# A batched matrix product in groups of four: neighbours, or one matrix from each quarter of the batch

## Chip, core and metric

The kernel runs on one core of a Trainium2 chip. The core has compute engines that run side by side: PE (matrix products and transposes), DVE (vector copies and casts), ACT (copies and casts as well), and POOL, which here only builds an identity matrix. SP does no arithmetic; it issues the transfers between the device's memory and the core's own memory, SBUF. Sixteen DMA engines carry the transfers out. SBUF has 128 partitions, and a tile is 128 rows, one in each partition. The metric is the device time in microseconds; less is better.

## The reference

128 independent products (8 x 16 matrices), each of a 256 x 512 matrix x with a 512 x 384 matrix of weights, all float32:

```python
b1, b2, m, k, n = 8, 16, 256, 512, 384
x:      (b1, b2, m, k)
weight: (b1, b2, k, n)

def reference(x, weight):
    return np.matmul(x, weight).astype(np.float32)
```

The kernel reads 67.1 MB of x and 100.7 MB of weights and writes 50.3 MB of output.

## The kernel before

The 128 matrices are taken in NG = 32 groups of G = 4. A group of before is four neighbours in memory. Three kinds of transfer serve one group:

- two weight loads, for two matrices each: 1,024 rows of weights stand one behind the other in memory and are cut into 128 runs of 8 rows (8 x 384 x 4 = 12,288 bytes), one run to a partition of `w_sb` (lines 103 to 108);
- one load of x: 1,024 rows, cut into 128 runs of 8 rows (8 x 512 x 4 = 16,384 bytes), into `x_sb` (lines 111 to 114);
- one store of the output, of 128 runs of 8 rows (8 x 384 x 4 = 12,288 bytes), from `out_sb` (line 122). The last group's store is cut in four pieces.

Thus partition p of `x_sb` has rows of matrix p // 32 of the group, and partition p of a weight slot has rows of matrix p // 64 of its pair.

The order is written out by hand. Each engine has its own program, and semaphores tie them together. SP (`on_sync`) issues the loads of the first four groups, then in turn the loads of group n + 4 and the store of group n. Before each it waits until the buffer is free: a weight slot when DVE has cast it (`w_cast`, line 102), an x slot when ACT has cast it (`x_cast`, line 110), and before a store until ACT has written the output tile (`o_copied`, line 121). There are 4 weight slots (two groups), 2 slots of x and 4 of output. A load into one of them can be issued as soon as the group two earlier has been cast.

ACT casts x to bfloat16 (`cast_x`, line 132), PE transposes it (line 166), DVE casts the weights (line 147) and copies the transposes out of PE's accumulation memory (line 153), PE multiplies (line 180) and ACT copies the product to `out_sb` (line 194). ACT's first copy of a group waits until the store of four groups earlier has read that output tile (`o_out`, line 192).

The lines that the change touches make the patterns of the transfers. The left one is in SBUF, the right one in memory:

```python
x_rows = x.rearrange("b1 b2 m k -> (b1 b2 m) k")
x_sb[s % XS][:]
x_rows[bass.ds(n * (G * M), G * M)].rearrange("(p r) k -> p r k", r=R)
```

A partition's rows follow each other on both sides, so the program has [128 runs, 4096 numbers] on each side of the load of x, and [128, 3072] on each side of the loads of weights and of the whole stores.

Of the kernel before, what the change touches and what calls it, by code (L numbers as in the profile page):

```python
# [12 lines left out]
def kernel(  # L13
# [9 lines left out]
    b1, b2, M, K = x.shape  # L23
    _, _, _, N = weight.shape
    B = b1 * b2
    KO = K // P

    x_rows = x.rearrange("b1 b2 m k -> (b1 b2 m) k")
    w_rows = weight.rearrange("b1 b2 k n -> (b1 b2 k) n")
    o_rows = out.rearrange("b1 b2 m n -> (b1 b2 m) n")  # L30

    fp32 = mybir.dt.float32
    bf16 = mybir.dt.bfloat16

# [5 lines left out]
    G = 4  # L40
    C = P // G
    R = G * M // P
    T = R // 2
    D = 2
    S = 2
    HP = P // D
    NG = B // G

    XS, WS, OS = 2, 2 * G // D, 4
    BS, TS, WBS = 1, 2, 2 * G  # L50
# [6 lines left out]
    def sbuf(name, shape, dtype, n):  # L57
        return [
            ctx.enter_context(nc.sbuf_tensor(f"{name}{s}", shape, dtype)) for s in range(n)
        ]  # L60
# [6 lines left out]
    def sems(name, n):  # L67
        return [tc.alloc_semaphore(f"{name}{s}") for s in range(n)]
# [3 lines left out]
    x_sb = sbuf("x_sb", [P, R, K], fp32, XS)  # L72
# [3 lines left out]
    w_sb = sbuf("w_sb", [P, S * KO, N], fp32, WS)  # L76
    w_bf = sbuf("w_bf", [P, KO, N], bf16, WBS)
    out_sb = sbuf("out_sb", [P, R, N], fp32, OS)
# [12 lines left out]
    x_in, w_in, o_out = sems("x_in", XS), sems("w_in", WS), sems("o_out", OS)  # L91
# [5 lines left out]
    def load(e, t, U, s):  # L97
        n = t * U + s
        for d in range(G // D):
            slot = (s * (G // D) + d) % WS  # L100
            if not isinstance(n, int) or n >= 2:
                e.wait_ge(w_cast, n * (G * S) + ((d + 1) * D * S - 2 * G * S))
            e.dma_start(  # L103
                w_sb[slot][:],
                w_rows[bass.ds(n * (G * K) + d * (D * K), D * K)].rearrange(
                    "(p k) n -> p k n", k=S * KO
                ),
            ).then_inc(w_in[slot], 16)
        if not isinstance(n, int) or n >= XS:
            e.wait_ge(x_cast, n * T + (1 - XS) * T)  # L110
        e.dma_start(  # L111
            x_sb[s % XS][:],
            x_rows[bass.ds(n * (G * M), G * M)].rearrange("(p r) k -> p r k", r=R),
        ).then_inc(x_in[s % XS], 16)

    def store(e, t, U, s, pieces=1):
        n = t * U + s
        dram = o_rows[bass.ds(n * (G * M), G * M)].rearrange("(p r) n -> p r n", r=R)
        for q in range(pieces):
            rows = slice(q * R // pieces, (q + 1) * R // pieces)  # L120
            e.wait_ge(o_copied, n * T + ((q + 1) * T // pieces + BIAS))
            e.dma_start(out=dram[:, rows], in_=out_sb[s % OS][:, rows]).then_inc(
                o_out[s % OS], 16
            )

    def cast_x(e, t, U, s, q):
        n = t * U + s
# [77 lines left out]
    def on_sync(e):  # L205
        U = OS
        for n in range(LAG):
            load(e, 0, NG, n)
        rounds = (NG - LAG) // U
        with e.Fori(0, rounds) as t:  # L210
            for s in range(U):
                load(e, t, U, LAG + s)
                store(e, t, U, s)
        for n in range(rounds * U, NG):
            if n + LAG < NG:
                load(e, 0, NG, n + LAG)
            store(e, 0, NG, n, T if n == NG - 1 else 1)
        for s in range(OS):
            e.wait_ge(o_out[s], 16 + 16 * (NG // OS + (T - 1 if s == (NG - 1) % OS else 0)))
# [67 lines left out]
```

## Time and profile before

| | |
|---|---|
| median of 3 runs | 518.51 us (518.35 to 518.73) |
| the profiled execution, whole | 518.98 us |
| its span, from the first to the last instruction | 517.2 us |
| moved | 218.18 MB, 422 GB/s over the span |
| PE busy | 306.6 us (59%) |
| DVE busy | 332.8 us (64%) |
| ACT busy | 236.7 us (46%) |

Times of the profile are those of one execution. A percentage is a share of the span. In the view of slices, the span is cut into 40 equal parts, and a digit is the busy share of a part in tenths, 9 for 90% or more; the row "DMA" is the mean over the sixteen DMA engines. A packet is what a DMA engine moves in one piece. In rows of waits, the engine and line that wait stand on the left, what ended the wait on the right, and then the time in total, the number of times and the longest. In rows of issues, the last number is the median time from the issue of a transfer to its landing. L103 is line 103 of the kernel before.

### The profile page before, as it was taken

How to read it: one execution, taken by the hardware profiler on the slowest of the kernel's cores; microseconds unless marked ns; L12 is line 12 of the kernel's file. 1: busy time of each engine (PE TensorE's matmuls, PEld its weight loads, DVE VectorE, ACT ScalarE, POOL GpSimd, SP SyncE). 2: the span in 40 equal slices, each digit the busy share in tenths (PEclk: the TensorE clock that was granted, in tenths of full speed). 3: DMA queues.
4: the chain of work that ended last, by engine and by line, in shares of the span. 5: the costliest groups of instructions: out<-in, count | busy, mean ns of one | idle time of the engine just before them, and what ended most of it. 6: DMA issues, size and time to landing. Idle time of an engine off the chain costs nothing.

```text
span 517.2 us, 11523 instructions
## 1 busy us (share of the span) xinstructions
PE 306.6 (59%) x4608; PEld 200.6 (39%) x4608; DVE 332.8 (64%) x384; ACT 236.7 (46%) x264; POOL 0.7 (0%) x6
## 2 busy tenths in 40 slices
PE   0478776556665457645577554776446765467752
PEld 0345444334443334433344332444324443244431
DVE  3698875667556676556675566855658656676550
ACT  0465564443644436435355354454444544544441
POOL 0000000000000000000000000000000000000000
PEclk9998877878777887878777778877788877778777
DMA  8999999999999999999999999999999999999996
GB/s 340 430 423 424 424 432 426 429 428 430 432 427 427 427 428 432 429 427 430 426 431 431 426 429 430 427 432 427 427 429 429 427 433 425 430 428 430 429 428 251
DMA packets 18869, 218.18 MB, mean 422 GB/s; under 512 B 2096, under 2 KB 2096, under 8 KB 2608
## 3 DMA queue, kind: packets, MB, share of 16 engines
q1 hardware_dynamic: 18864, 218.11, 99.3%
q8 instruction: 3, 0.05, 0.0%
q14 instruction: 2, 0.02, 0.0%
HBM read 167.77 MB, written 50.33 MB: 422 GB/s over the span
## 4 chain that ended last, share of the span: by engine, by line
DMA 81%; ACT 10%; PE 4%; issue 3%; ACTq 0%; SPq 0%
DMA x_sb<-in_x_dram 81%; ACT x_bf L132 9%; PE po L180 2%; PE pt L166 1%; ACTq L130 0%; ACT out_sb L194 0%; SPq L111 0%; SPq L103 0%; ACT L132 0%; ACTq L193 0%; SPq L282 0%; SPq L55 0%
## 5 line engine op out<-in xcount | busy, mean ns | idle before, releaser
L147 DVE CAST w_bf<-w_sb 64x1536 bf16<-64x1536 f32 x256 | 244.4, 955 | 47.2 <-DMA w_sb<-in_weight_dram 38.5
L166 PE MATMUL pt<-identity,x_bf 128*128 128x128 f32 x512 | 123.7, 425 | 199.3 <-ACT x_bf L132 199.1
L180 PE MATMUL po<-w_bf,x_t 128*32 128x384 bf16 x4096 | 185.1, 342 | 1.0 <-issue 1.0
L166 PEld LDWEIGHTS pt<-identity,x_bf 128*128 128x128 f32 x512 | 91.8, 216 | 232.1 <-issue 218.3
L194 ACT COPY out_sb<-po 128x768 f32<-128x768 f32 x128 | 102.2, 798 | 147.2 <-PE po L180 147.2
L153 DVE COPY x_t<-pt 128x1024 bf16<-128x1024 bf16 x128 | 88.4, 691 | 122.3 <-PE pt L166 121.8
L132 ACT CAST x_bf<-x_sb 128x1024 bf16<-128x1024 f32 x128 | 124.4, 1042 | 80.9 <-DMA x_sb<-in_x_dram 80.8
L180 PEld LDWEIGHTS po<-w_bf,x_t 128*32 128x32 bf16 x4096 | 108.8, 101 | 73.8 <-issue 14.2
L132 ACT ACT_TABLE_LOAD x8 | 10.3, 1283 | 42.9 <-DMA x_sb<-in_x_dram 42.9
masks.py:199 POOL TENSOR_SCALAR_AFFINE_SELECT identity<-identity 128x128 f32<-128x128 f32 x1 | 0.3, 292 | 0.2 <-POOL identity L200 0.2
L200 POOL MEMSET identity<- 128x128 f32 x1 | 0.2, 204 | 0.5 <-SPq L55 0.5
L271 POOL MEMSET const-bfloat16-1.0<- 128x1 bf16 x1 | 0.1, 101 | 0.0
L271 POOL MEMSET const-uint8-127<- 128x1 uint8 x1 | 0.1, 101 | 0.0
L271 POOL MEMSET const-float32-0.0<- 128x1 f32 x1 | 0.1, 98 | 0.2 <-issue 0.2
L271 POOL MEMSET const-float32-1.0<- 128x1 f32 x1 | 0.1, 98 | 0.0
## 6 DMA issues: line engine op xcount, KB each, us to landing
w_sb<-in_weight_dram SPq DMA_DIRECT2D x64, 1536.0 KB, 27.5
x_sb<-in_x_dram SPq DMA_DIRECT2D x32, 2048.0 KB, 27.5
out_dram<-out_sb SPq DMA_DIRECT2D x31, 1536.0 KB, 30.7
out_dram<-out_sb SPq DMA_DIRECT2D x4, 384.0 KB, 5.9
```

Source lines behind the costliest of these rows:

```text
L132: e.copy(out=x_bf[s % BS][:, rows], in_=x_sb[s % XS][:, rows].rearrange("p r (q s c) -> p r s q c", s=S, c=KO),).then_inc(x_cast, 1)
L147: e.tensor_copy(out=w_bf[(s * G + d * D + a) % WBS][h * HP : (h + 1) * HP], in_=w_sb[slot][a * HP : (a + 1) * HP, h * KO : (h + 1) * KO, : ...
L153: e.tensor_copy(out=x_t[s % TS][:, 2 * q : 2 * q + 2], in_=pt[(s * T + q) % PT][:].bitcast(bf16),).then_inc(t_copied, 1)
L166: ins = e.transpose(pt[(s * T + q) % PT][:, rr, h, :], words[:, 2 * q + rr, h :: KO // 2], identity[:],)
L180: ins = e.matmul(po[(s * T + q) % PO][mine, rr, :N], x_t[s % TS][:, 2 * q + rr, ko // 2, mine, ko % 2], w_bf[(s * G + i) % WBS][:, ko, :], ...
L194: e.copy(out=out_sb[s % OS][:, 2 * q : 2 * q + 2, :], in_=po[(s * T + q) % PO][:, :, :N],).then_inc(o_copied, 1)
L200: e.memset(identity[:], 0.0).then_inc(id_done, 1)
L271: nc = _bacc.Bacc("TRN2", target_bir_lowering=False, num_devices=1)
```

## The change

A group is now made of matrices n, n + 32, n + 64 and n + 96, one from each quarter of the batch. The memory of x, weights and output is named in four dimensions (quarter i, group n, run within the matrix, bytes of the run), and a transfer takes all quarters (for weights: two of four) at one n. The runs of a matrix keep their length and partition; only which matrices stand in a group is new, and where the transfers go in memory. The quarters begin 16.8 MB apart in x, 25.2 MB in the weights and 12.6 MB in the output. The product, the casts, the waits and the order of issues are as they were; the lines after the new ones move down by up to seven.

```diff
-    x_rows = x.rearrange("b1 b2 m k -> (b1 b2 m) k")
-    w_rows = weight.rearrange("b1 b2 k n -> (b1 b2 k) n")
-    o_rows = out.rearrange("b1 b2 m n -> (b1 b2 m) n")
...
+    x_runs = x.rearrange("b1 b2 m k -> (b1 b2 m) k").rearrange(
+        "(i n c r) k -> i n c (r k)", i=G, n=NG, r=R
+    )
+    w_runs = weight.rearrange("b1 b2 k n -> (b1 b2 k) n").rearrange(
+        "(i n p k) f -> i n p (k f)", i=G, n=NG, k=S * KO
+    )
+    o_runs = out.rearrange("b1 b2 m n -> (b1 b2 m) n").rearrange(
+        "(i n c r) f -> i n c (r f)", i=G, n=NG, r=R
+    )
...
             e.dma_start(
-                w_sb[slot][:],
-                w_rows[bass.ds(n * (G * K) + d * (D * K), D * K)].rearrange(
-                    "(p k) n -> p k n", k=S * KO
+                w_sb[slot][:].rearrange("p k n -> p (k n)"),
+                w_runs[d * D : (d + 1) * D, bass.ds(n, 1)].rearrange(
+                    "i n p f -> i (n p) f"
                 ),
             ).then_inc(w_in[slot], 16)
...
         e.dma_start(
-            x_sb[s % XS][:],
-            x_rows[bass.ds(n * (G * M), G * M)].rearrange("(p r) k -> p r k", r=R),
+            x_sb[s % XS][:].rearrange("p r k -> p (r k)"),
+            x_runs[:, bass.ds(n, 1)].rearrange("i n c f -> i (n c) f"),
         ).then_inc(x_in[s % XS], 16)
...
-        dram = o_rows[bass.ds(n * (G * M), G * M)].rearrange("(p r) n -> p r n", r=R)
+        dram = o_runs[:, bass.ds(n, 1)].rearrange("i n c f -> i (n c) f")
         for q in range(pieces):
-            rows = slice(q * R // pieces, (q + 1) * R // pieces)
+            run = slice(q * R * N // pieces, (q + 1) * R * N // pieces)
             e.wait_ge(o_copied, n * T + ((q + 1) * T // pieces + BIAS))
-            e.dma_start(out=dram[:, rows], in_=out_sb[s % OS][:, rows]).then_inc(
-                o_out[s % OS], 16
-            )
+            e.dma_start(
+                out=dram[:, :, run],
+                in_=out_sb[s % OS][:].rearrange("p r n -> p (r n)")[:, run],
+            ).then_inc(o_out[s % OS], 16)
```

## The prediction

> **What bounds the kernel now.** I read the slices of the page first, then the DMA queues, one stretch of the middle, the waits of the queue that issues the transfers (SP), and the issues. The slices, with the queue under them:
>
> ```profile
> DMA  8999999999999999999999999999999999999996
> GB/s 340 430 423 424 424 432 426 429 428 430 432 427 427 427 428 432 429 427 430 426 431 431 426 429 430 427 432 427 427 429 429 427 433 425 430 428 430 429 428 251
> DMA packets 18869, 218.18 MB, mean 422 GB/s; under 512 B 2096, under 2 KB 2096, under 8 KB 2608
> ## 3 DMA queue, kind: packets, MB, share of 16 engines
> q1 hardware_dynamic: 18864, 218.11, 99.3%
> ```
>
> The sixteen DMA engines are full from the first slice to the last but one, so the time is bytes over engines. I take one price from these lines: 99.3% of 16 engines over 517.2 us is 8217 engine-us for 218.11 MB, or 37.67 engine-us per MB (26.5 GB/s for one engine). A row of 12,288 B then holds its engine for 0.463 us, one of 16,384 B for 0.617 us. The work of one engine of the sixteen is 8217/16 = 513.6 us; the span has 3.6 us besides, for start and end. One stretch of the middle, two groups long (columns: busy us of PE, PE loads, DVE, ACT and POOL with counts, clock, DMA share, GB/s), says the same without the ends:
>
> ```profile
> 200.00:264.00 64.00, 39.01 (x582) 25.39 (x584) 41.76 (x50) 29.60 (x33) 0.00 (x0) 0.79 1.01 429
> ```
>
> 429 GB/s over 16 is 26.8 GB/s an engine, and DVE, the busiest of the compute engines, works 41.8 of 64 us. The packet count shows how a transfer is cut: 64 weight loads, 32 x loads and 35 stores are 131 transfers; at 128 rows each that is 16,768 packets, and the 2096 under 512 B are 131 x 16, one completion from each of sixteen engines. 16,768 + 2096 = 18,864, the queue's count. So a packet is one row of one partition, and every transfer is shared by all sixteen engines, 8 rows each.
>
> ```profile
> SPq L103 <- DVE w_bf L147: 269.5, 60, 8.6
> SPq L111 <- ACT x_bf L132: 122.5, 30, 5.6
> SPq L122 <- ACT out_sb L194: 35.5, 6, 16.2
> ```
>
> (waits of SP's queue: us in total, times, longest) and, from the issues (KB each, median us from issue to landing):
>
> ```profile
> w_sb<-in_weight_dram SPq DMA_DIRECT2D x64, 1536.0 KB, 27.5
> x_sb<-in_x_dram SPq DMA_DIRECT2D x32, 2048.0 KB, 27.5
> out_dram<-out_sb SPq DMA_DIRECT2D x31, 1536.0 KB, 30.7
> ```
>
> SP waits for buffers to be emptied by the casts, and still a transfer takes 27.5 us from issue to landing although its own 8 rows need 3.7 us: it stands behind some two groups of other transfers. That backlog is why SP's waits cost nothing.
>
> [...] a transfer issued from SP runs on k engines, [...] The trace before agrees for 128 against 128: k = 16, by the 2096 completions. No trace before shows a smaller k. [...]
>
> **The change part by part.** Instruction order and counts of PE, DVE, ACT and SP stay as they are; the built program differs in the shapes of the transfers alone. Bytes and row sizes stay too: 12,288 B rows of weight and output, 16,384 B rows of x. Costs nothing: which four matrices make a group, since no instruction of the casts, transposes or products sees it.
>
> What changes is the pattern on the DRAM side. Four matrices of four quarters don't follow each other in memory, so the rows no longer make one dimension of 128. The weight load is [2, 64, 3072] against [128, 1, 3072] in SBUF, the x load [4, 32, 4096] against [128, 1, 4096], the store [4, 32, 3072] against [128, 3072]. [...] k is 2 for the weight loads, 4 for x loads and stores. Engines 0 and 1 then carry half of every weight load and a quarter of everything else; 2 and 3 a quarter of x and output; twelve carry nothing. For engine 0:
>
> - weights: 64 loads x 64 rows = 4096 rows, 50.33 MB x 37.67 = 1896 us
> - x: 32 loads x 32 rows = 1024 rows, 16.78 MB x 37.67 = 632 us
> - output: a quarter of 50.33 MB, 12.58 MB x 37.67 = 474 us
> - sum 79.69 MB, 3002 us, against 513.6 now.
>
> Does engine 0 stay full? A group is 59.3 + 19.8 + 14.8 = 93.8 us of it. From the rows of the page, DVE needs 8 x 0.955 + 4 x 0.691 = 10.4 us a group, ACT 4 x (1.042 + 0.798) = 7.4, PE 306.6/32 = 9.6. A weight slot is cast within 4 x 0.955 us and its next load issued while the other slots' loads, worth more than 60 us, wait behind the engine. So compute hides under the transfers, and SP's waits still cost nothing, longer as they get. Twelve idle engines hide nothing, since no row may move to them. At the end, the last x share is followed on engine 0 by four stores of 14.8 us; the last group's compute takes 11 us (first cast at 496.66, last copy out at 507.72), and its first copy out waits for the first of those stores (four output buffers); so the last pieces join before the engine runs dry. Start and end stay 3.6 us: span 3006.
>
> An unknown: [...] Bounds: from below nothing, if an engine's own pace is the limit or they don't meet. From above, engines 0 and 1 in step through all x and output rows, each at half pace: 632 + 474 = 1106 us more. I take one meeting a group, costing engine 1 once [...] 4 x 0.463 = 1.85 us, 32 times, 59 us. [...] Another unknown is the pace of an engine alone: the best slice, 433 GB/s or 27.1 an engine, makes 2945 of the 3002[...].
>
> Sum: 3006 + 59 = 3065 for the span. The profiled execution took 518.98 for a span of 517.2, 1.8 around it; its 518.98 stands 0.5 above the median of 518.51, which at this size is nothing. Forecast 3067 us.
>
> **The rivals.**
> - *All sixteen engines stay* (not slower). Place: the cut of a transfer into shares. If the 128 partitions on the SBUF side alone decide it, or the two DRAM dimensions are walked as one before sharing, each engine keeps 8 rows and 513.6 us; price nothing, time 518.5. For it: packets follow partitions today, and the rows keep their size. [...] It decides if the x loads show 16 completions. 4 in 100.
> - *Sixteen engines, but far regions collide in HBM* [...] The quarters lie 16.8 MB apart in x, 25.2 in weights, 12.6 in output. At half rate: 2 x 513.6 + 5.4, about 1033 us. Against: inside a quarter 32 or 64 rows follow each other[...]. 3 in 100.
> - *In step [...]*: above 3350, up to 3006 + 1106 + 2 = 4114 us. For it: engines 0 and 1 get the same list at the same time. Against: nothing holds them in step. 8 in 100.
> - *Shares handed out one engine after the other*: [...] nearly all 218.11 MB go in series, up to 8217 us. The trace shows only shares of 8 rows, so it can't exclude this. 2 in 100.
> - *A lone engine is faster than 26.8 GB/s*, if today's pace is a share of a common limit: at twice the pace, 1500 us. Against: the slices hold 423 to 433 whatever mix of loads and stores they have. 2 in 100.
>
> **How the numbers follow.** The forecast's own case [...] has 81 in 100: from 2950 (best slice's pace, no meeting) to 3350 (a quarter of the in-step cost, 277, over the 59). The rest lies outside, 8 above [...], 2 far above, 9 below; so the range is 2950 to 3350. A measurement here tells 0.2% from no change. Slower: 81 + 8 + 3 + 2 + 2 = 96. Of the rival with sixteen engines 3 are within 0.2%, and 1 is faster, by some packets that wait less.
>
> **What would show it.** In the changed profile: DMA share near 3002 x 2 + (632 + 474) x 2 over 16 x 3065, some 17% (tenths of 1 or 2); about 71 GB/s; completions of 64 x 2 + 67 x 4 = 396 in place of 2096, so about 17,170 packets in all; weight loads landing 100 us or more after issue; DVE busy the same 333 us but 11% of the span. Wrong would be 2096 completions (then a sixteen-engine rival), a DMA share well under 17% (shares in series, or an engine that runs dry), or a queue time per MB far from 37.67 ([...] a faster lone engine).

## The result, and the profile after

The changed kernel took 3352.85 us (3335.56 to 3375.89, six runs) where the kernel before took 518.29 in the runs beside it: 6.4686 times as long, 95% interval 6.4408 to 6.4965. The forecast was 3067, its range 2950 to 3350. The direction and the main cause were right; a term beside the main sum was too small by a factor of six to seven, and the time lies just past the end of the range.

From the page of the changed kernel, the slices and the queue under them:

```profile
DMA  1111111211111111221112111111111121111121
GB/s 61 61 65 51 60 65 68 66 54 63 66 69 72 55 63 63 70 70 55 66 65 70 70 57 67 65 69 73 60 66 64 68 70 65 68 60 65 68 70 78
DMA packets 17169, 218.17 MB, mean 65 GB/s; under 512 B 396, under 2 KB 396, under 8 KB 908
## 3 DMA queue, kind: packets, MB, share of 16 engines
q1 hardware_dynamic: 17164, 218.11, 18.0%
```

The bytes are the same, but the sixteen engines are busy for 18.0% where it was 99.3%, and 422 GB/s have become 65. The packets under 512 B, the completions, went from 2096 to 396. That is exactly 64 x 2 + 67 x 4: a weight load runs on two engines, a load of x and a store on four. The page gives no time to landing for these transfers, and its chain puts 88% down to an unknown queue. As I read it, both say that the transfers' ends weren't matched; the packets are the place to look.

DVE waits for weights 2325.8 of the 3355 us, and SP no longer shows many waits (the first line is DVE's, the second SP's):

```profile
DVE w_bf L154 <- DMA w_sb<-in_weight_dram: 2325.8, 64, 44.2
```

```profile
SPq L109 <- DVE w_bf L154: 96.9, 4, 38.2
```

Before, SP waited 269.5 us at that place. It isn't free now: it is held inside the issue itself. One load of x, by its tile, before and after (min/median/max in ns):

```profile
L111 SPq DMA_DIRECT2D x_sb<-in_x_dram x32: 328/333/483, 1.9 to 468.9; - x32
```

```profile
L117 SPq DMA_DIRECT2D x_sb<-in_x_dram x32: 7337/28462/29877, 2.3 to 3188.6; - x32
```

An issue of 0.33 us has become one of 28 us. Why it takes so long the trace doesn't show; when it ends, engine 1 (as named below) has 70 to 74 rows left before its own x in twelve of the first thirteen groups. The end of the issue goes with the start on engines 2 and 3: in the first seven groups their first row of x starts 0.8 to 0.9 us after it.

What the sum of 3006 left out shows in single rows, a row being the packet of one partition. The packet records of the trace have no engine number, but each row starts where the last one on its engine ended, so they can be put into four chains. Two of them have weights and are engines 0 and 1, two have none and are engines 2 and 3. Which is which of a pair the records don't say, nor to which partitions a row goes: the numbers are names, and I call engine 1 the one whose weights are slowed. From the first twelve to thirteen groups of the changed kernel, mean ns of a row:

```
                     weights (12,288 B)   x (16,384 B)   output (12,288 B)
engine 0                  473                 614               494
engine 1                  559                 644               460
engine 2                   -                 1054               463
engine 3                   -                 1085               466
two_halves, median        460                 611               460
```

The last line is from the run on two engines below (two_halves); it stands for a row alone. Engine 1's weight rows take 99 ns longer than that; over its 4096 such rows it would be 0.41 ms. Engines 2 and 3 take 1.7 to 1.8 times as long for a row of x. Engine 0, which reads from the same far regions, loses 13 ns a weight row. It is engine 1 that sets the time: up to 1400 us its chain has gaps of 0.3 us in all, while engine 0 stands idle for 121 us. Many of the slow rows take near two or three times the time alone, others fall between. Here is the second group's second weight load on engine 1, four rows to a line (start in us, ns of each), with the x of engine 2 (or 3) beside it:

```
engine 1, second weight load                  engine 2 (or 3), x
120.60   621 1245  460  460                   117.04   869 1302  781 1199
123.37   632 1349 1367 1289                   121.18  1347 1227 1749 1828
128.00   800 1351 1349 1382                   127.32  1149 1675 1834 1552
132.87   789  945 1369 1349                   133.51  1180 1802 1628  725
137.30   954  804 1213 1349                   138.84  1079 1792 1274  611
141.61  1081  812 1053 1359                   143.58  1061 1801 1255  611
145.90  1066  468  838 1053                   148.29  1066 1628 1199  855
149.31  1066  468  460  460                   153.03   655 1211 1219  724
151.75   460  466  460  460
```

The first 32 rows took 31.2 us, where 32 x 0.457 would be 14.6 (0.457 us is the step from one start to the next). The view of the queue in that stretch, 90 to 210 us in slices of 3 us, shows it as bytes:

```profile
DMA  1111111112222221222222111111111122222222
GB/s 56 53 53 53 53 53 57 53 59 91 67 63 64 59 64 53 68 72 61 67 74 83 57 57 49 57 52 56 52 56 56 51 75 86 86 91 81 86 96 78
```

From the start two engines are busy and move 53 GB/s, 26.7 each. From the tenth slice on (117 us) it is up to four, and from 120 to 156 us they move 53 to 83, not 107. By the chains engine 0 keeps its 26.7 from 120.6 to 151.8 us, while engines 1, 2 and 3 move 12.6, 12.6 and 12.1: the three together 1.4 times what one moves alone. The next x of engines 2 and 3 begins at 188 us; there the loss is smaller (75 to 96).

The start at 117 us follows from SP. Its timeline (start and duration in us) has the issue of this load of x end at 116.2 us, and engine 2's first row of it starts at 117.0:

```profile
86.90 29.27 SPq L117 DMA_DIRECT2D x_sb<-in_x_dram  x1
```

### The profile page after: what moved, and what is told of

It is laid out like the page before. It is cut to its first block, busy times and chain, and to the rows that moved or that the text cites. A ratio compares the mean times of both kernels' runs of the same rounds, so it can differ in the third digit from the quotient of the medians.

```text
span 3355.0 us, 11523 instructions
## 1 busy us (share of the span) xinstructions
PE 365.7 (11%) x4608; PEld 224.4 (7%) x4608; DVE 332.8 (10%) x384; ACT 234.1 (7%) x264; POOL 0.7 (0%) x6
## 2 busy tenths in 40 slices
DMA packets 17169, 218.17 MB, mean 65 GB/s; under 512 B 396, under 2 KB 396, under 8 KB 908
## 4 chain that ended last, share of the span: by engine, by line
another core or an unknown queue 88%; PE 5%; ACT 4%; issue 1%; ACTq 0%; SPq 0%
PE po L187 5%; ACT x_bf L139 3%; ACT out_sb L201 1%; PE pt L173 0%; ACTq L137 0%; ACTq L200 0%; ACTq L252 0%; ACT L139 0%; ACTq L250 0%; ACTq L289 0%; SPq L61 0%; ACTq L248 0%
## 5 line engine op out<-in xcount | busy, mean ns | idle before, releaser
L154 DVE CAST w_bf<-w_sb 64x1536 bf16<-64x1536 f32 x256 | 244.4, 955 | 2331.8 <-DMA w_sb<-in_weight_dram 2325.8
L187 PE MATMUL po<-w_bf,x_t 128*32 128x384 bf16 x4096 | 242.8, 407 | 197.7 <-ACT out_sb L201 197.7
L187 PEld LDWEIGHTS po<-w_bf,x_t 128*32 128x32 bf16 x4096 | 131.7, 118 | 303.9 <-issue 218.0
```

Of the source, the lines that this page charges most:

```text
L154: e.tensor_copy(out=w_bf[(s * G + d * D + a) % WBS][h * HP : (h + 1) * HP], in_=w_sb[slot][a * HP : (a + 1) * HP, h * KO : (h + 1) * KO, : ...
L187: ins = e.matmul(po[(s * T + q) % PO][mine, rr, :N], x_t[s % TS][:, 2 * q + rr, ko // 2, mine, ko % 2], w_bf[(s * G + i) % WBS][:, ko, :], ...
```

## The experiments

**Regions: matrices two apart.** Only the addresses change; the patterns keep their leading dimensions. `t * (U // 2) + s // 2` is the pair of groups, `s % 2` the one in it.

```diff
-        "(i n c r) k -> i n c (r k)", i=G, n=NG, r=R
+        "(j i u c r) k -> i j u c (r k)", i=G, u=2, j=NG // 2, r=R
...
-            x_runs[:, bass.ds(n, 1)].rearrange("i n c f -> i (n c) f"),
+            x_runs[:, bass.ds(t * (U // 2) + s // 2, 1), s % 2].rearrange("i n c f -> i (n c) f"),
```

> The four matrices of a group stand two matrices apart (1.0 MB in x, 1.6 MB in the weights, 0.8 MB in the output) instead of a quarter of the batch; the patterns keep their leading dimensions of 2 and 4, so shares and engines stay those of the changed kernel. If the engines' shares [...] set the time: 3350, within 50. If the far regions cost the 350 us over the sum of 3006: nearer 3006, at most 3100.

Measured: 3356.18 us (3353.68 and 3358.68), the changed kernel's time. How far apart the regions lie, a quarter of the batch or two matrices, doesn't matter here. Common to both is that the matrices of a group no longer follow each other, so that their rows don't make one dimension.

**Two engines for everything: two halves of the batch.**

```diff
-        "(i n c r) k -> i n c (r k)", i=G, n=NG, r=R
+        "(i n c r) k -> i n c (r k)", i=2, n=NG, r=R
...
-        "(i n p k) f -> i n p (k f)", i=G, n=NG, k=S * KO
+        "(i n d p k) f -> d i n p (k f)", i=2, n=NG, d=2, k=S * KO
...
-                        out=w_bf[(s * G + d * D + a) % WBS][h * HP : (h + 1) * HP],
+                        out=w_bf[(s * G + a * D + d) % WBS][h * HP : (h + 1) * HP],
```

> A group takes two neighbours from each half of the batch, so that every transfer, x and output too, has a leading dimension of 2: engines 0 and 1 carry 109 MB each, [...] 109.05 MB x 37.67 + 6 = 4114, within 20, and a queue price of 37.7 engine-us per MB. Far regions or a slow lone engine as the cause: the price stays at the changed kernel's 44 (18.0% of 16 x 3355 over 218.11 MB), 4830.

Measured: 4063.18 us, and in the queue

```profile
q1 hardware_dynamic: 17030, 218.10, 12.6%
```

12.6% of 16 x 4061.2 us over 218.10 MB is 37.5 engine-us per MB, against 44 for the changed kernel. Rows of weights and output took 461 ns on average, rows of x 613. So far regions and two engines leave the pace of an engine as it was (0.463 and 0.617 us a row by the price before), and the changed kernel's dearer rows need something that this run lacks. The time was 51 us under the forecast. Some 30 of it is that rows overlap by about 4 ns at their ends, over 8,500 packets an engine, which the share counts twice; most of the rest is that rows took 2 ns less than in the kernel before. The span less 6 us, allowed for start and end, makes 37.2 per MB. At that pace the changed kernel's engine 0 or 1 needs 79.69 x 37.2 + 6 = 2971, and 3355 - 2971 = 384 us are to be explained.

**Far groups on sixteen engines.** The same four quarters, but patterns with 32 or 128 outermost: x by runs first, weights and stores by single matrices. A matrix of weights then goes to all 128 partitions in rows of 6,144 B, the casts follow that order, and PE takes every fourth column of the transposed x.

```diff
-            x_runs[:, bass.ds(n, 1)].rearrange("i n c f -> i (n c) f"),
+            x_runs[:, bass.ds(n, 1)].rearrange("i n c f -> (n c) i f"),
...
+            for a in range(D):
+                e.dma_start(
+                    w_sb[slot][:, a * KO : (a + 1) * KO].rearrange("p k n -> p (k n)"),
+                    w_runs[d * D + a, bass.ds(n, 1)].rearrange("n p f -> (n p) f"),
+                ).then_inc(w_in[slot], 16)
...
-                            x_t[s % TS][:, 2 * q + rr, ko // 2, mine, ko % 2],
+                            x_t[s % TS][:, 2 * q + rr, ko // 2, i::G, ko % 2],
...
+            for i in (0, 2, 1, 3):
+                e.dma_start(
+                    out=dram[i, :, run],
+                    in_=out_sb[s % OS][i * C : (i + 1) * C].rearrange("p r n -> p (r n)")[:, run],
+                ).then_inc(o_out[s % OS], 16)
```

> The far groups stay, but each transfer is cut [...]: x by runs first (32 runs x 4 quarters against 128 partitions, so partition 4c+i has run c of quarter i), the weights by single matrices over 128 partitions (rows of 6144 B), the stores by single matrices of 32 partitions. Loss of engines as the cause of nearly all: back to 519 for loads, and up to 118 more [...]: 520 to 640. Far regions colliding in HBM: 1000 or more.

Measured: 528.16 us, ratio to the kernel before 1.0182 (1.0165 to 1.0199).

```profile
DMA packets 29765, 218.19 MB, mean 413 GB/s; under 512 B 4800, under 2 KB 4800, under 8 KB 21696
## 3 DMA queue, kind: packets, MB, share of 16 engines
q1 hardware_dynamic: 29760, 218.12, 99.9%
```

4800 completions are 300 transfers on 16 engines each, and the queue is full again. The same groups from the same far regions cost 10 us, not 2.8 ms: the loss came with the cut to two and four engines.

**The same cut, from neighbours.** To tell whether those 10 us are the regions:

```diff
-        "(i n c r) k -> i n c (r k)", i=G, n=NG, r=R
+        "(n i c r) k -> i n c (r k)", i=G, n=NG, r=R
```

(and so for weights and output)

> The far16 kernel's transfers, cut the same way, but from four neighbours, as before the change. If the 10 us that far16 lies above the kernel before come from the cut (more and smaller rows, stores of 32 partitions): the same as far16, 528 within 2. If they come from the far regions: 518 to 520.

Measured: 529.18 us, 1.0209 (1.0192 to 1.0227). No better from neighbours, so the 10 us belong to the cut, and the far regions cost nothing that can be seen here.

**Sixteen engines, weights to half of the partitions at a time.** Against far16 the weight loads differ, with the casts that follow them: a matrix goes to 64 partitions, in rows of 12,288 B again.

```diff
-                    w_sb[slot][:, a * KO : (a + 1) * KO].rearrange("p k n -> p (k n)"),
+                    w_sb[slot][a * HP : (a + 1) * HP].rearrange("p k n -> p (k n)"),
```

> As the far16 kernel, but each weight load of a matrix goes to 64 partitions (rows of 12,288 B), [...] 100.66 MB at twice the price, 37.67 x 100.66 / 16 = 237 us more than far16, 700 to 880. If only the count of engines matters: the same as far16, within 15.

Measured: 764.25 us, 236 more than far16, where twice the price for the weights' bytes makes 237.

```profile
q1 hardware_dynamic: 21568, 218.12, 98.8%
```

The queue looks full, as in far16, while it moves 287 GB/s. A busy engine in this view is one that has a row under way, not one that moves at its pace. Rows of 12,288 B took 726 ns on average, most of those for weights 0.83 to 0.98 us.

**Engines 2 and 3 without x.** The changed kernel, with half of x left out (POOL first sets that half of its tiles to zero, which the lines below don't show):

```diff
-            x_sb[s % XS][:].rearrange("p r k -> p (r k)"),
-            x_runs[:, bass.ds(n, 1)].rearrange("i n c f -> i (n c) f"),
+            x_sb[s % XS][: 2 * C].rearrange("p r k -> p (r k)"),
+            x_runs[:2, bass.ds(n, 1)].rearrange("i n c f -> i (n c) f"),
```

> The changed kernel with x of quarters 0 and 1 alone loaded (partitions 64 to 127 of x stay zero, so half of the output isn't computed from x). Engines 0 and 1 carry the same 79.69 MB as in the changed kernel, engines 2 and 3 only stores. At the pace of the two_halves run (37.2 engine-us per MB) that is 2965 + 6 = 2971. [...] engines 0 and 1 out of step: 2971 to 3050. Then nothing delays engine 1 any more, and if the two stay in step [...]: above 3350, up to 2971 + 624 + 468 = 4063. [...] between 2971 and 3350, by the share of the bytes left out.

Measured: 2989.05 us, 364 less than the changed kernel, though engines 0 and 1 do the same work in both, and close to 2971.

```profile
q1 hardware_dynamic: 15052, 184.55, 15.1%
```

So the 384 us are nearly all what engines 2 and 3 do to engine 1 with their x. By the chains, up to 1000 us, engine 1's weight rows take 462 ns here where they took 559. Most of the 18 us left over is engines 0 and 1 meeting each other: they begin x at 61.8 and 62.2 us in the first group and hinder each other, which costs engine 1 some 15 us in two groups; by the fourth they begin at 309.0 and 311.3, that is 2.3 us apart where it was 0.4. Where the rows of engines 1, 2 and 3 meet wasn't shown. The author's estimate is that it is in SBUF, where several engines write the same half of the partitions. For it are half_ports, where only the partitions and the length of the weights' rows changed (236 us), and engine 0, which reads from the same far regions, beside the same transfers, and loses 13 ns a weight row to engine 1's 99. A changed kernel with the x of engines 2 and 3 in the other half of the partitions wasn't run.

**One part at a time**, on the kernel before: the pattern of the weight loads alone, of the loads of x alone, of the stores alone, each as in the change's diff.

> The kernel before with the weight loads alone taken from quarters (x and output go to neighbours, so the products mix matrices). Engines 0 and 1 carry 50.33 MB of weights and a sixteenth of x and output, 57.67 MB: 2145 + 6 = 2151, and up to 80 more [...]. If the count of engines were not the cause: 519.

> The kernel before with the loads of x alone taken from quarters (the products mix matrices). Engines 0 to 3 carry 16.78 MB of x and a sixteenth of the rest, 26.22 MB: 975 + 6 = 981. If engines 0 and 1, and 2 and 3, stay in step [...], up to 624 more: 1605.

> The kernel before with the stores alone going to quarters (results land in the places of other matrices). Engines 0 to 3 carry 12.58 MB of output and a sixteenth of the rest, 23.07 MB: 858 + 6 = 864. In step [...], up to 468 more: 1332.

Measured: 2265.08, 1101.56 (a second run took 1119.79) and 893.00 us, where the sums without meetings were 2151, 981 and 864. The ranking is that of the bytes per engine: weights on two engines cost most, stores on four least. All three lie above their sum, by 114, 121 and 29 us, the weights by more than the 80 I had allowed; none comes near the bound of engines in step (1605 for x, 1332 for stores). How the meetings divide in these three I didn't follow.

## Why the prediction was right or wrong

- *The patterns set the engines, 2 for weights and 4 for x and output.* Right, to the packet: 396 completions, 17,169 packets against 17,170. The step from the pattern to k, the number of engines, was taken ahead of any trace of it. This case shows k = 2 and k = 4 for 2 and 4 outermost in memory (396 completions), and far16 shows 16 for 32 against 128 (4800); for other patterns it wasn't shown.
- *Engine 0 carries 79.69 MB, 3002 us.* Right within 1.3%: at the pace of two_halves it is 2965.
- *Engine 0 or 1 stays full, compute hides.* Right in effect: x_half ends 18 us over the bare sum, and in the changed kernel engine 1 never runs dry. Wrong of engine 0, which stood idle for 121 us up to 1400, about 9 us a group, while engine 1 was behind. That "SP's waits" would only get longer was wrong in form: SP is held in its issues.
- *Far regions.* Priced at nothing in the forecast, with a rival of 3 in 100; near2 (3356 us beside 3353) and near16 (529 beside 528) bear that out.
- *The meeting, 59 us.* This is the step that failed. It read: "I take one meeting a group", at "4 x 0.463 = 1.85 us". There is one meeting a group, with engine 1, as it says; but it doesn't end after four rows. By the runs it is worth 384 us in all, 364 of them by x_half, or 11 to 12 us a group. Two things were missing. Engines 2 and 3 stand idle before each load of x and begin together every time, in the first fourteen groups within 0.3 us of each other, while engines 0 and 1 drift apart (x_half: from 0.4 to 2.3 us in four groups). And they begin beside engine 1: in the chains, their x began 2 to 4 us before engine 1's second weight load in twelve of the thirteen groups followed (117.0 and 120.6 us, 601.5 and 605.5, 1032.6 and 1036.6), when engine 1 had some 70 rows left before its own x. The three then move side by side, in the stretch above each at just under half its pace (12 to 13 GB/s of 26.7). That SP's issue puts them there is what the chains suggest (0.8 to 0.9 us from its end to their first row); no run moved it. The prediction called a queue time per MB far from 37.67 a sign that it was wrong, and that did show: 44 engine-us per MB.
- *The range.* Its upper end took "a quarter of the in-step cost" of engines 0 and 1, the pair that x_half shows falling out of step. The pair that stays in step, 2 and 3, wasn't priced at all, because it isn't the slowest; it is the one that slows the slowest. The time of 3353 lies just inside the rival *in step*, but that rival had engines 0 and 1 in step, and its mechanism isn't what the runs show.

## What to carry to other kernels

Before you change addresses, write down the two outermost dimensions of each transfer as the instruction will carry them: if rows stop making one dimension, a transfer can fall from 16 engines to 2, and the completions on the page count it. Count also what the other engines do meanwhile: one that has little to move can still slow the one that sets the time (here the x of engines 2 and 3 was worth 364 us), again in each round if it starts at the same place. And where four far matrices are wanted, put the runs outermost and the matrices inside, or move single matrices, as far16 does: 528 us instead of 3353.

## What the runs showed of the hardware

- The time of a slowed row is often near a multiple of the time alone, with many between: in the changed kernel near 460 and 1360 ns for 12,288 B, and near 611, 1210 and 1810 ns for 16,384 B. With the weights of a matrix in 64 partitions instead of 128 (half_ports), and rows of 12,288 B instead of 6,144, sixteen engines took 236 us more than in far16, where twice the cost of the weights makes 237.
- An issue of a load of x on SP took 28 us at the median in the changed kernel, where engine 1 had some 70 rows still to move when it ended, against 0.33 us before.
- Stores of 32 partitions were allowed 118 us more, an estimate that no run bears out; with all else in the cut, far16 lost 10. Two stores in turn read opposite halves of the partitions there; whether that is why wasn't tested.
- The granted clock of PE fell from 0.803 to 0.563 with PE busy for 11% of the span instead of 59%. It cost nothing that shows here: x_half, at a clock of 0.572, ends 18 us over the sum of the transfers alone.
